# Down projection of a SwiGLU layer: four passes over two column blocks and half the rows, with some row tiles by seven products

## The chip, the cores and the metric

The kernel runs on one core of one Trainium2 chip. TensorE (PE) multiplies; VectorE (DVE) and ScalarE (ACT) prepare its operands and take its results out of PSUM; SyncE (SP) issues the loads of the weights, GpSimd (POOL) some other transfers. The time is that of one execution on the device, in microseconds. Three executions of the kernel before took 1140.74 (the median), 1136.53 and 1142.36.

## The reference

One decoder layer over 256 tokens of width 2048, in float32. The part that matters here is the feed-forward part with D_FF = 5632, and what surrounds it:

```python
x = x + mixed @ w_o[i]
hf = rms_norm(x, g_ffn_norm[i])
x = x + (jax.nn.silu(hf @ w_gate[i]) * (hf @ w_up[i])) @ w_down[i]
gate = jax.nn.sigmoid(rms_norm(x, g_ple_norm[i]) @ w_ple_gate[i])
x = x + gate * (p[i] @ w_ple_proj[i])
```

`w_down` is 5632 x 2048: 44 row tiles of 128 rows, and four column blocks of 512 columns.

## The kernel before, in words

**Products.** To keep float32 accuracy, each operand is split into a rounded high part and the rest (`w_hi`, `w_lo`; `gh`, `gl` for the gated values). A product of two such operands takes three matmuls: high by high, high by low, low by high. Tokens come as two tiles of 128 (t = 0, 1).

**Weights.** The class `Weights` cuts every weight matrix into chunks of two row tiles by up to 512 columns (512 KB), in the order in which they are used. `load_to` (line 163 on) issues the loads on SP, in order; a chunk goes into one of five buffers `raw`, or, of certain numbers below `more_end`, into one of two more buffers `w_more`. `split_to` makes `w_hi` on ACT (L200) and `w_lo` on DVE (L201); there are three buffers of each (PART). `take` keeps the splits and the loads ahead of the products.

**Seven products.** In gate/up, a chunk of `w_gate` and the chunk of `w_up` of the same rows form a pair. A pair of ordinary chunks needs eight block products of three matmuls. The up chunks in `W.mixed` are handled by `mix` (L206 on): sums of the four blocks of the pair (`w_sum`, L216), which are split (`w_last`, `w_mix`, L219 and L220), and `pair` (L1420) then makes seven block products in place of eight, with sums of the left operand (`rows`, made by `row_sums`, L1084). Four of the seven go into four shared PSUM banks (`pp_p`), the others into the four accumulators. `shared` (L1451) combines the four banks after the last such pair of a block, and the accumulators are added to that at the end of the block. In each of the 11 blocks of gate/up, four of eight pairs are of this kind (three in the first). Two sets of sum buffers (NSET) stand ready.

**Down.** Each of the four column blocks of `w_down` is one call of `block`: 22 chunks, each of 12 matmuls, into two of the four accumulators, so that the next block can start in the other two. Before the first chunks, `need_g` splits the gated values `gr` into `gh` and `gl`. After a block, `residual` (L1290) adds the accumulators to the tokens `xs`, and `norm_task` squares them, transposes them by PE and splits them into `ph`, `pl` for the last product (`ple`), between which and down lies the small product of `p` (`pp`).

**Order of the work.** The kernel is written as one list; a planner puts it in order for each engine at build time by simulated times and priorities. `high_priority` moves instructions ahead: the splits of the weights by 70 (W_AHEAD), the end of a gate/up block by 100 (G_AHEAD); the norm is put back by 100 (AHEAD). On the chip each engine then runs its own list in order, waiting on semaphores.

**Space.** Beside the weights' buffers there are 39 slots of 4 KB a partition (`S`), handed out first in, first out, and four PSUM banks (`PP`) beside the four accumulators.

## Time and profile before

| what | us |
|---|---|
| median of three runs | 1140.74 |
| lowest, highest | 1136.53, 1142.36 |
| the profiled execution's own time | 1135.29 |
| its span, first to last instruction | 1133.2 |
| gate/up blocks, from about | 320 to 785 |
| down blocks | 785 to 1028 |
| p product and last product | 1028 to 1128 |

The profile is of one execution. PE, DVE, ACT, POOL are busy times; PEld is the loading of the left operand, which runs beside the matmuls. Matmuls overlap, so one shows 0.39 us though the next starts after 0.23: a rate is read from the distance of starts. "L201" is line 201 of the kernel. A wait is written as who waited, and for whom: `DVE w_lo L201 <- ACT w_hi L200`. In the tables by stretch, each engine's busy time is followed by its number of instructions; then come the clock granted to PE (1.00 is full), the share of the DMA engines and GB/s.

### The profile page before, as it was taken

The numbers are of one execution on the slowest core, as the hardware profiler recorded it, in microseconds if no ns is written. First come the engines' busy times: TensorE is split into PE (matmuls) and PEld (weight loads), VectorE is DVE, ScalarE is ACT, GpSimd is POOL, SyncE is SP. The second block draws the span as 40 slices with busy tenths as digits, with TensorE's granted clock in tenths as the row PEclk, the third lists the DMA queues.
The fourth block names the chain that finished last, engine by engine and source line by source line (L and its number), as shares of the span: only waits on it lengthen the run. The fifth ranks groups of instructions, "written<-read, shape, count | busy, mean of one in ns | idle before, by whom it ended". The sixth has DMA issues, their size and how long they took to land.

```text
span 1133.2 us, 15659 instructions
## 1 busy us (share of the span) xinstructions
PE 1112.5 (98%) x5809; PEld 919.6 (81%) x5809; DVE 899.2 (79%) x1304; ACT 664.6 (59%) x946; POOL 23.3 (2%) x48
## 2 busy tenths in 40 slices
PE   9999999999999999999999999999999999999998
PEld 6877877889887878887887888888888888888886
DVE  7989998658799999999999999999744454546554
ACT  7864994636675766666665665667444343436443
POOL 1000020000000000000000000000000000000000
PEclk9999999999999999999999999999999999999999
DMA  9996470356685666666666665766665655555662
GB/s 336 242 271 202 115 237 23 108 189 201 194 275 180 196 196 185 211 201 183 212 201 183 217 204 176 223 218 198 197 193 187 195 188 192 186 195 187 211 212 86
DMA packets 113340, 221.16 MB, mean 195 GB/s; under 512 B 8160, under 2 KB 13040, under 8 KB 113264
## 3 DMA queue, kind: packets, MB, share of 16 engines
q1 hardware_dynamic: 109808, 211.23, 59.3%
q0 software_dynamic: 3456, 8.94, 2.5%
q8 instruction: 45, 0.74, 0.3%
q14 instruction: 31, 0.25, 0.1%
HBM read 214.76 MB, written 5.37 MB: 194 GB/s over the span
## 4 chain that ended last, share of the span: by engine, by line
PE 56%; DVE 28%; issue 6%; DMA 5%; ACT 3%; DVEq 0%; POOL 0%; SPq 0%; ACTq 0%; POOLq 0%
PE acc L371 48%; DVE w_lo L201 9%; DVE w_sum L216 7%; DMA w_raw<-in_w_up_dram 3%; DVE w_mix L220 3%; PE pp_p L371 3%; DVE uc L355 2%; DVE w_last L220 2%; DVE wsg L355 1%; DMA e<-in_bE_dram 1%; PE pp_at L371 1%; DVE w L763 1%; ACT w_hi L200 1%; PE pp_at L1016 1%; PE pp_v L744 1%
## 5 line engine op out<-in xcount | busy, mean ns | idle before, releaser
L201 DVE TENSOR_TENSOR w_lo<-w_raw,w_hi 128x1024 fp32r<-128x1024 f32 (+2 forms) x302 | 362.6, 1205 | 185.7 <-ACT w_hi L200 185.2
L200 ACT ACTIVATE w_hi<-w_raw 128x1024 fp32r<-128x1024 f32 (+2 forms) x302 | 314.6, 1044 | 291.1 <-PE acc L371 257.9
L371 PE MATMUL acc<-w_hi,fh 128*128 128x512 f32 x403 | 159.7, 396 | 0.1
L371 PE MATMUL acc<-w_lo,fh 128*128 128x512 f32 x403 | 158.3, 393 | 0.8
L371 PE MATMUL acc<-w_hi,fl 128*128 128x512 f32 x403 | 157.4, 391 | 0.0
L371 PE MATMUL acc<-w_hi,gh 128*128 128x512 f32 x352 | 137.6, 391 | 0.1
L371 PE MATMUL acc<-w_lo,gh 128*128 128x512 f32 x352 | 136.9, 389 | 0.0
L371 PE MATMUL acc<-w_hi,gl 128*128 128x512 f32 x352 | 136.9, 389 | 0.0
L219 ACT ACTIVATE w_mix<-w_sum 128x1024 fp32r<-128x1024 f32 x86 | 91.0, 1058 | 70.5 <-DVE w_sum L216 69.4
L220 DVE TENSOR_TENSOR w_mix<-w_sum,w_mix 128x1024 fp32r<-128x1024 f32 x86 | 104.8, 1219 | 0.3 <-ACT w_mix L219 0.2
L371 PE MATMUL pp_p<-w_mix,sum 128*128 128x512 f32 x387 | 95.3, 390 | 2.0 <-DVE fl L363 2.0
L371 PEld LDWEIGHTS acc<-w_lo,fh 128*128 128x128 f32 x403 | 76.0, 188 | 18.4 <-DVE w_lo L201 3.5
L371 PEld LDWEIGHTS acc<-w_hi,fh 128*128 128x128 f32 x403 | 75.8, 188 | 16.8 <-DVE uc L355 1.7
L371 PEld LDWEIGHTS acc<-w_hi,fl 128*128 128x128 f32 x403 | 75.9, 188 | 15.7
L371 PEld LDWEIGHTS pp_p<-w_mix,sum 128*128 128x128 f32 x387 | 72.4, 188 | 17.9 <-issue 2.4
L371 PEld LDWEIGHTS acc<-w_hi,gh 128*128 128x128 f32 x352 | 66.1, 188 | 14.0 <-DVE uc L355 0.4
L371 PEld LDWEIGHTS acc<-w_hi,gl 128*128 128x128 f32 x352 | 66.1, 188 | 13.8
L371 PEld LDWEIGHTS acc<-w_lo,gh 128*128 128x128 f32 x352 | 66.1, 188 | 13.7
L371 PE MATMUL acc<-w_hi,ph 128*128 128x512 f32 x128 | 49.8, 389 | 0.0
L371 PE MATMUL acc<-w_lo,ph 128*128 128x512 f32 x128 | 49.8, 389 | 0.0
L371 PE MATMUL acc<-w_hi,pl 128*128 128x512 f32 x128 | 49.8, 389 | 0.0
L200 ACT ACTIVATE w_hi<-w_more 128x1024 fp32r<-128x1024 f32 x37 | 39.0, 1054 | 14.5 <-PE acc L371 5.7
(318 smaller groups left out, 1906.9 us busy)
## 6 DMA issues: line engine op xcount, KB each, us to landing
w_raw<-in_w_down_dram SPq DMA_DIRECT2D x88, 512.0 KB, 4.3
w_raw<-in_w_gate_dram SPq DMA_DIRECT2D x64, 512.0 KB, 4.4
w_raw<-in_w_up_dram SPq DMA_DIRECT2D x63, 512.0 KB, 4.7
w_raw<-in_w_o_dram SPq DMA_DIRECT2D x32, 512.0 KB, 3.8
w_raw<-in_w_ple_gate_dram SPq DMA_DIRECT2D x32, 512.0 KB, 4.2
w_more<-in_w_up_dram SPq DMA_DIRECT2D x25, 512.0 KB, 4.6
w_raw<-in_w_in_dram SPq DMA_DIRECT2D x24, 512.0 KB, 7.7
w_more<-in_w_gate_dram SPq DMA_DIRECT2D x24, 512.0 KB, 4.3
```

The source lines that it names most:

```text
L200: self.nc.scalar.activation(out=hi, in_=raw, func=AF.Copy)
L201: self.nc.vector.tensor_tensor(out=lo, in0=raw, in1=hi.bitcast(F32), op=ALU.subtract)
L216: V.tensor_tensor(out=o, in0=a, in1=b, op=ALU.add)
L219: A.activation(out=h, in_=r, func=AF.Copy)
L220: V.tensor_tensor(out=l, in0=r, in1=h.bitcast(F32), op=ALU.subtract)
L355: V.tensor_tensor(out=o, in0=a, in1=b, op=op)
L371: T.matmul(out=o, lhsT=a, rhs=b, start=start, stop=stop)
L744: T.matmul(out=pv[p, r * 256 + i4 * 64:r * 256 + i4 * 64 + 64], lhsT=ee[r][p, i * 64:i * 64 + 64], rhs=um[p, i, :], start=True, stop=True, ...
L763: V.tensor_tensor_scan(out=w, data0=dc, data1=w, initial=0.0, op0=ALU.mult, op1=ALU.add)
L1016: T.matmul(out=o, lhsT=a, rhs=b_, start=False, stop=(i == 1), skip_group_check=True)
```

## The change

The down projection is computed by `mixed_block`, as gate/up is. There are four passes: for the first 20 row tiles (the first five gated tiles of four) the column blocks 0 and 1 together, then 2 and 3 together; then the same for the other 24 row tiles. A pair is two chunks of the same rows in two neighbouring column blocks. In each of two column pairs, seven of the 22 pairs of row tiles (D_MIXED: 3, 5, 8 in the first half, 13, 15, 17, 20 in the second) use seven products: 14 of 44. The gated values of a half are split when it comes up, and with them the sums of rows for the pairs in D_MIXED (`split_g`). Each pass uses all four accumulators, and ends with four combinations (`ws`, `uc`) and four additions to `xs`, so each column block is added to `xs` twice. The norm follows passes 2 and 3, for two column blocks at a time. The two `w_more` buffers are used up to the loads of gate/up block 8 only and their slots given back at block 9; gate 0 is split before block 10; the buffers of the sums are kept to the last pass.

```diff
-    blk["down"] = [W.block(w_down, 0, 44, 512 * b, 512) for b in range(4)]
+    D_MIXED, D_SPLIT = (3, 5, 8, 13, 15, 17, 20), 5
+    blk["down"] = []
+    for half in (range(2 * D_SPLIT), range(2 * D_SPLIT, 22)):
+        for p in range(2):
+            ids = [(j, *(W.block(w_down, 2 * j, 2, 1024 * p + c, 512)[0] for c in (0, 512))) for j in half]
+            W.mixed.update(i[2] for i in ids if i[0] in D_MIXED)
+            blk["down"].append(ids)
...
-    W.more_end = blk["down"][0][0]
+    W.more_end = blk["gu"][8][0][1]
     W.more.extend(wait_n(2, [128, 2, 512], "w_more"))
+    more = list(W.more)
     gr, gh, gl = [], [], []
+    lhs_g = tiles4(gh, gl)
...
     for b in range(11):
+        if b == 9:
+            S.put(*more)
+        if b == 10:
+            W.more.clear()
+            gh.append(wait_get([128, 4, 256], "gh", F32R))
+            gl.append(wait_get([128, 4, 256], "gl", F32R))
+            split(gh[0], gl[0], gr[0])
+            S.put(gr[0])
         ws = wsg[b % 2]
         acc = mixed_block(blk["gu"][b], lhs_f, rows, ws, uc, need_f)
...
-    S.put(*more, *fh, *fl, *rows.values(), uc, *w_sum)
-    for last, _, parts in W.sums:
-        S.put(last, *parts[0], *parts[1])
+    S.put(*fh, *fl, *rows.values(), wsg[1])
     for i in range(4):
         xs[i // 2][i % 2] = t = wait_get([128, 1024], "xs")
         nc.gpsimd.dma_start(out=t, in_=keep[i])
-    lhs_g = tiles4(gh, gl)
-
-    def need_g(k):
-        while len(gh) <= min(k // 4 + 1, 10):
+    rows = {}
+
+    def need_g(j):
+        last = D_SPLIT if j < 2 * D_SPLIT else 11
+        if n == 1 and j == 2 * D_SPLIT - 3:
+            split_g(D_SPLIT + 1)
+        split_g(min((j + 1) // 2 + 1, last))
+
+    def split_g(m):
+        while len(gh) < m:
             i = len(gh)
             sched.until(f"g{i}")
             gh.append(wait_get([128, 4, 256], "gh", F32R))
             gl.append(wait_get([128, 4, 256], "gl", F32R))
             split(gh[i], gl[i], gr[i])
+            for q in range(2):
+                if 2 * i + q in D_MIXED:
+                    w = wait_get([128, 512], "rows")
+                    o = rows[2 * i + q] = wait_get([128, 2, 512], "sum", F32R)
+                    row_sums((w, o[:, 0], o[:, 1]), gr[i][:, 2 * q:2 * q + 2].rearrange("p k n -> p (k n)"))
+                    S.put(w)
             S.put(gr[i])
...
-    for b in range(4):
-        ph.append(wait_get([128, 4, 256], "ph", F32R))
-        pl.append(wait_get([128, 4, 256], "pl", F32R))
-        acc = block(blk["down"][b], lhs_g, need_g)
-        residual(acc, r_f, b)
-        sched.add(norm_task(xv, b, ss_p, ph, pl, G_PLE, "hp"), 0)
-        if b == 0:
-            S.put(*wsg)
+    ws = wsg[0]
+    for n, ids in enumerate(blk["down"]):
+        p, h = n % 2, n // 2
+        acc = mixed_block(ids, lhs_g, rows, ws, uc, need_g)
+        with tc.high_priority(G_AHEAD):
+            for t in range(2):
+                tt(ws[:, t], ws[:, t], acc[2 * t], ALU.add)
+            for t in range(2):
+                tt(uc[:, t], acc[2 * t + 1], uc[:, t], ALU.subtract)
+        for c, o in enumerate((ws, uc)):
+            for t in range(2):
+                stt(xv(t, 2 * p + c), o[:, t], r_f[:, t:t + 1], xv(t, 2 * p + c))
+        if n == 3:
+            S.put(*gh[D_SPLIT:], *gl[D_SPLIT:], *(rows[j] for j in D_MIXED if j >= 2 * D_SPLIT), *w_sum)
+            for last, _, parts in W.sums:
+                S.put(last, *parts[0], *parts[1])
+        if h:
+            for b in (2 * p, 2 * p + 1):
+                ph.append(wait_get([128, 4, 256], "ph", F32R))
+                pl.append(wait_get([128, 4, 256], "pl", F32R))
+                sched.add(norm_task(xv, b, ss_p, ph, pl, G_PLE, "hp"), 0)
+        if n == 1:
+            S.put(*gh[:D_SPLIT], *gl[:D_SPLIT], *(rows[j] for j in D_MIXED if j < 2 * D_SPLIT))
+            pr_ = wait_get([128, 2, 2, 256], "prhl", F32R)
+            prh, prl = pr_[:, 0], pr_[:, 1]
             pr32 = wait_get([128, 2, 256], "pr32")
             nc.gpsimd.dma_start(out=pr32, in_=pT)
...
```

## The prediction, made before the changed kernel was run

> **What bounds the kernel now.** First the page: the engines' totals.

> ```profile
> span 1133.2 us, 15659 instructions
> PE 1112.5 (98%) x5809; PEld 919.6 (81%) x5809; DVE 899.2 (79%) x1304; ACT 664.6 (59%) x946; POOL 23.3 (2%) x48
> ```

> TensorE is busy in nearly the whole span, and VectorE for 79% of it. An average over stages hides which of the two is near its limit where, so next the busy time of each engine in stretches: two gate/up blocks of 42 us, then the four down blocks (columns: length, then PE, PEld, DVE, ACT, POOL).

> ```profile
> 414.00:456.00 42.00, 42.00 (x190) 34.49 (x188) 40.71 (x51) 26.26 (x30) 0.00 (x0) 1.00 0.65 198
> 456.00:498.00 42.00, 41.87 (x188) 34.11 (x187) 40.56 (x51) 26.23 (x30) 0.00 (x0) 1.00 0.64 198
> 785.00:846.00 61.00, 60.92 (x273) 50.05 (x272) 39.92 (x38) 26.62 (x28) 0.00 (x0) 1.00 0.59 188
> 846.00:907.00 61.00, 61.00 (x275) 50.57 (x274) 30.10 (x30) 26.02 (x30) 0.00 (x0) 1.00 0.60 191
> 907.00:968.00 61.00, 61.00 (x275) 50.57 (x274) 30.26 (x30) 26.02 (x30) 0.00 (x0) 1.00 0.59 191
> ```

> In gate/up, where four of eight pairs already use seven products, DVE is 97% busy (40.7 of 42). In down it is half idle (30 of 61). So down is bound by PE alone, and the change spends DVE's idle time there to save PE work. Third, the chain of waits in order of time gives the rates, because overlapping instructions show longer durations than their distance (columns: start, us, what).

> ```profile
> 623.09 1.14 DVE w_mix L220
> 627.10 1.20 DVE w_sum L216 x2
> 657.70 1.20 DVE uc L355 x2
> 742.26 1.21 DVE uc L355 x2
> 794.84 57.17 PE acc L371 x252
> 852.01 0.87 PE pp_n L398 x8
> 852.89 59.89 PE acc L371 x264
> ```

> A matmul of 512 columns takes 57.17/252 = 0.2269 us, a transpose 0.87/8 = 0.109. A 1024-wide DVE operation takes 1.14, a 512-wide one 0.60. A gate/up block lasts (742.26 - 657.70)/2 = 42.28 us (two periods lie between these rows); its PE work is 4x21 + 4x24 = 180 matmuls and 8 transposes, 41.71. A block at 97% DVE thus loses 0.57 us, while 264 down matmuls run without a gap.

> **The matmuls removed.** A pair by seven products has 21 matmuls, an ordinary one 24. That the form does so on the chip is in the page:

> ```profile
> L371 PE MATMUL pp_p<-w_mix,sum 128*128 128x512 f32 x387 | 95.3, 390 | 2.0 <-DVE fl L363 2.0
> L219 ACT ACTIVATE w_mix<-w_sum 128x1024 fp32r<-128x1024 f32 x86 | 91.0, 1058 | 70.5 <-DVE w_sum L216 69.4
> L220 DVE TENSOR_TENSOR w_mix<-w_sum,w_mix 128x1024 fp32r<-128x1024 f32 x86 | 104.8, 1219 | 0.3 <-ACT w_mix L219 0.2
> ```

> 86/2 = 43 pairs, 387/43 = 9 matmuls of three shared products each. Fourteen pairs save 14 x 3 = 42 matmuls, 42 x 0.2269 = **-9.53 us**. [...]

> **DVE in the four passes.** Each new pair replaces one ordinary split (1.14) by four sums, one half split and two splits: 5 x 0.60 + 2 x 1.14 = 5.28. Further rows:

> ```profile
> 1028.42 1.40 DVE L363 SCALAR_TENSOR_TENSOR xs<-acc,r_f,xs 128x512 f32<-128x512 f32 x2
> 1036.63 1.65 DVE L363 SCALAR_TENSOR_TENSOR pl<-pp_n,gc,ph 128x256 fp32r<-128x256 f32 x4
> L355 DVE TENSOR_TENSOR rows<-rows x16: 281/283/293, 304.3 to 340.3; 128x128 f32<-128x128 f32 x16
> L355 DVE TENSOR_TENSOR gl<-g,gh x11: 1219/1220/1222, 777.3 to 804.0; 128x1024 fp32r<-128x1024 f32 x11
> ```

> Residual 0.70 an operation, norm's lower half 0.41, a 128-wide sum about 0.21 (0.28 less the 0.07 by which the durations above exceed the distances); so row sums cost 4 x 0.21 + 0.60 = 1.44 for each of seven k positions. Each pass also has four shared sums (2.4) and, at its end, four combinations and four residuals (5.2), which run beside the next pass. The residual is made eight times more than before: +5.6 on DVE, under PE.
> - Pass 0: 17 split chunks 19.4, three mixes 15.8, shared 2.4, four gate splits 4.6, three row sums 4.3, block 10's end 3.6: 50.1. PE: 231 matmuls and 8 transposes, 53.3.
> - Pass 1: 19.4 + 15.8 + 2.4 + 5.2 + 1.1 (gate 5) + 0.6 (p) = 44.5. PE 52.4.
> - Pass 2: 20 chunks 22.8, four mixes 21.1, 2.4, 5.2, five gate splits 5.7, four row sums 5.8: 63.0. PE: 276 matmuls, 62.6.
> - Pass 3: 22.8 + 21.1 + 2.4 + 5.2 + 3.3 (norm of two column blocks) = 54.8. PE with 16 transposes 64.4.

> ACT has three copies of at most 1.06 and one of half the width in a new pair, 3.7 of its 4.8 us of PE, and less elsewhere, so DVE decides. Pass 2 alone asks for more than PE. Its relief: gate splits are planned as soon as their slots are free. The last row shows all eleven done by 804, while their block ran to 846. In pass 2 they take slots of gates 0 to 4, which pass 1 reads one after another, so some splits can move into pass 1 (8 us spare).

> **Stalls in the passes.** The trace has no such pass. Each is built like a gate/up block: all four accumulators in use, an ordinary pair last, ordinary pairs first, so that two of the accumulators are taken out while the last products still run. Nearest row: 0.57 a block. The bounds are 0 (down now) and 0.57 each for passes 0, 1 and 3; for pass 2 additionally 63.0/0.97 - 62.6 = 2.3 if nothing moves. I take 4 x 0.57 + 1.0 = **+3.3**, against at most 4.6.

> **The prefetch buffers.** `w_more` lends two buffers to the five of `raw`; the new limit stops it before block 8, since the 39 slots are full in block 10 (27 held by the stage, ten gates, two for `gh[0]` and `gl[0]`). Three blocks then mix at 97% DVE with five buffers. SP's loads wait for buffers, and DVE hardly for loads:

> ```profile
> SPq L174 <- DVE w_sum L216: 206.3, 70, 7.2
> SPq L174 <- DVE w_lo L201: 158.7, 93, 4.2
> DVE w_sum L216 <- DMA w_raw<-in_w_up_dram: 7.6, 8, 1.7
> DVE w_sum L216 <- DMA w_more<-in_w_up_dram: 1.1, 2, 0.6
> w_raw<-in_w_up_dram SPq DMA_DIRECT2D x63, 512.0 KB, 4.7
> ```

> One load shows what the two buffers do, the up chunk of a block's first mixed pair (instructions in order of time):

> ```profile
> 648.06 0.37 SPq L174 DMA_DIRECT2D w_more<-in_w_up_dram  x1
> 650.93 1.23 DVE L201 TENSOR_TENSOR w_lo<-w_raw,w_hi 128x1024 fp32r<-128x1024 f32 x1 [0.63 <-ACT w_hi L200]
> 652.81 0.69 DVE L216 TENSOR_TENSOR w_sum<-w_raw,w_more 128x512 f32<-128x512 f32 x1 [0.65 <-DMA w_more<-in_w_up_dram]
> ```

> It is used the moment it lands. Its pair starts two ordinary pairs (10.9) and the transposes (0.9) after the block's last accumulator is out (657.70 + 1.20), near 671, so 18 us later. With five buffers its issue waits for the chunk five before, whose last reader is the split ending at 652.16: it lands at 656.9, 4.1 us later. Queued behind it on SP are the next loads, on DVE its sums and those of the next mixed pair (they share `w_sum`). But DVE then has the block's ten end operations (6 us) to do, and the pair has 14 us left. DVE's spare is 3.3% of 42.28, 1.4 a block, so the bounds are 0 and 4.1 - 1.4 = 2.7 in each of three blocks, 0 to 8.1. DMA waits now cost DVE 8.7/11 = 0.8 a block; I let as much again arise and half reach PE: 3 x 0.4 = **+1.2**.

> **At no cost.** Bytes and size of the loads stay; POOL's reload of `xs` (four of 512 KB) and of `pT` lie 50 us before their use. The early split of gate 0 (1.14) falls into block 10, where four such splits fit already. The weight order changes between the column blocks only. The first new pair of pass 3 takes the four banks that norm uses, but 16.3 us into the pass (three ordinary pairs); norm's 3.3 on DVE is through by then. The end of down is the tight place:

> ```profile
> 1028.30:1040.00 11.70, 11.70 (x57) 9.77 (x56) 9.80 (x25) 10.30 (x19) 0.00 (x0) 1.00 0.60 195
> L367 ACT ACTIVATE pp_n<-xs 128x512 f32<-128x512 f32 x8 | 4.7, 582 | 0.0
> L367 ACT ACTIVATE ph<-pp_n,gc 128x256 fp32r<-128x256 f32 x12 | 4.7, 470 | 0.0
> ```

> ACT has 10.3 of 11.7 there, and gets two squares (0.58) and four copies (0.47) more, 3.0, since the last pass ends two column blocks at once. Their result isn't needed until eight row tiles into the last product, 10.9 after the p product. If the p product's own evictions are queued behind it, 10.3 + 3.0 - 11.7 = 1.6 is lost; I take **+0.3**, nearer to the cover.

> Sum: -9.53 + 3.3 + 1.2 + 0.3 = **-4.7 us**. The profiled execution took 1135.29 (span 1133.2 and 2.1 around it), which would become 1130.6. The three runs' median is 1140.74, 5.4 above it and within their spread of 1136.53 to 1142.36; on that scale the forecast is **1136.0**.

> **Rivals.**
> - *Clean (B).* The planner keeps DVE ahead throughout: stalls as in down now, 1 us in all. For it: passes 0, 1 and 3 are 85 to 94% full, below gate/up. Against: pass 2. Net -8.5: 1132.2.
> - *DVE sets the pace (C).* The seven-product pairs are there, but the saving becomes waiting: pass 2 +2.3, four ends 2.3, prefetch 3.0, tail 1.0; net -0.9: 1139.8. For it: DVE at 97 to 100%.
> - *Slower (D).* A stall long enough to slow PE's clock. The only large stall of gate/up shows it (PE in order of time; then one stretch: length, PE busy, granted clock, DMA share, GB/s):

> ```profile
> 340.82 0.39 PE L371 MATMUL acc<-w_hi,fl 128*128 128x512 f32 x1
> 343.26 0.93 PE L371 MATMUL pp_p<-w_mix,sum 128*128 128x512 f32 x3 [2.04 <-DVE fl L363]
> 345.58 0.63 PE L371 MATMUL acc<-w_hi,fl 128*128 128x512 f32 x1
> 346.00 0.63 PE L371 MATMUL pp_p<-w_hi,fh 128*128 128x512 f32 x1
> 344.60:348.00 3.40, 3.40 (x10) 0.51 0.09 9
> ```

> A distance of 2.44 instead of 0.23, and then 3.4 us at clock 0.51, in which half the work is lost: 2.2 + 1.7 = 3.9. Place: the mixed pairs of blocks 8, 9 and 10, whose sums come late with five buffers, and pass 2. One such stall in each is four, 15.6 in place of my 1.2 and 1.0: net +8.7, 1149.4. Without those two terms the sum is -6.9, so two stalls (+7.8) already make it slower than before, three give +4.8, four more than 0.5%. Against: 14 us of lead. [...] The trace halved the clock after a gap of 2.04, and D stays as priced.

> **How the numbers follow.** A measurement here tells about 0.5% (5.7 us) from no change. Forecast: 0.46; with stalls between 2.5 and 7 it spans -7 to -2.5 (1133.7 to 1138.2), and about 0.17 of it lies beyond -5.7. B 0.25, C 0.12, D 0.17. Faster 0.17 + 0.25 = 0.42; same 0.29 + 0.12 = 0.41; slower 0.17. The range takes in B and C, 3 us of the runs' spread below B, and D as far as three stalls (1145.5): 1129 to 1146.

> **What would show it.** Right: 42 fewer matmuls, down's matmuls ending about 5 us earlier counted from its first; DVE near 40 of 42 still in blocks 8 to 10, and no longer half idle but about 90% busy in the passes; no PE gap over 1 us. Wrong: PE waiting for `w_last` or `w_mix` behind DMA in blocks 8 to 10 (prefetch term), for `gl` or `sum` in pass 2 (pass term), clock below 1 between 400 us and the end of down (D), or gate/up blocks 8 to 10 as long as before and passes without gaps (B).

## The result, and the profile after

| | before | after |
|---|---|---|
| median of five runs (before: the first three stand above), us | 1140.74 | 1129.09 |
| lowest, highest | 1136.53, 1142.36 | 1126.46, 1130.01 |
| ratio after/before, 95% interval | | 0.9906 [0.9879, 0.9933] |
| profiled execution (span) | 1135.29 (1133.2) | 1129.42 (1127.7) |

The change makes the kernel about 0.9% faster. The medians are 11.65 us apart, the two profiled executions 5.9. A second series with 29 runs of the kernel before (after_again, below) gives a ratio of 0.9926 [0.9908, 0.9943]; of its median 1138.67 that is -8.4 us. That is the best figure of the three; why they differ is told further down.

First the engines' totals on the page of the kernel after, and the group of the shared products.

```profile
span 1127.7 us, 15773 instructions
PE 1103.1 (98%) x5767; PEld 911.7 (81%) x5767; DVE 987.9 (88%) x1463; ACT 692.8 (61%) x989; POOL 23.3 (2%) x48
L377 PE MATMUL pp_p<-w_mix,sum 128*128 128x512 f32 x513 | 126.4, 390 | 1.6 <-DVE fl L369 1.1
```

There are 42 matmuls fewer (5809 to 5767) and 513/9 = 57 pairs by seven products, 43 + 14. DVE has 89 us more to do, ACT 28. Where the time went is read from two groups of matmuls, that of gate/up (`fh`) and that of down (`gh`): count, durations, and the first and the last start. First of the kernel before, then of the kernel after.

```profile
L371 PE MATMUL acc<-w_hi,fh x403: 387/389/632, 315.7 to 784.5; 128*128 128x512 f32 x135
L371 PE MATMUL acc<-w_hi,gh x352: 389/389/497, 785.2 to 1028.0; 128*128 128x512 f32 x176
```

```profile
L377 PE MATMUL acc<-w_hi,fh x403: 387/389/500, 318.5 to 786.4; 128*128 128x512 f32 x135
L377 PE MATMUL acc<-w_hi,gh x254: 389/389/496, 787.1 to 1021.7; 128*128 128x512 f32 x127
```

Down, counted from its first to its last `gh` matmul, takes 234.6 us in place of 242.8: **-8.2**. (The expectations below count to the first matmul of the p product, 0.7 later.) Gate/up, from its first matmul to down's first, takes 468.6 in place of 469.5. From the last `gh` matmul to the end of the span there are 106.0 in place of 105.2. In the part ahead of gate/up, which the change does not touch, the kernel after happened to be slower: its first `fh` matmul starts at 318.5 in place of 315.7. That is why the two profiled executions lie only 5.9 apart. Now stretches of the kernel after: one gate/up block (block 8), then the four passes. Columns: length, then PE, PEld, DVE, ACT, POOL, each with its number of instructions; PE's clock, DMA share, GB/s.

```profile
667.00:709.00 42.00, 41.73 (x188) 34.28 (x187) 40.70 (x50) 26.27 (x30) 0.00 (x0) 1.00 0.63 197
...
787.00:840.00 53.00, 53.00 (x239) 43.81 (x238) 50.98 (x66) 31.33 (x36) 0.53 (x1) 1.00 0.63 209
840.00:893.00 53.00, 53.00 (x236) 43.89 (x235) 48.36 (x69) 31.75 (x36) 0.54 (x1) 1.00 0.62 203
893.00:957.00 64.00, 62.52 (x276) 51.44 (x275) 58.89 (x69) 34.79 (x39) 0.00 (x0) 1.00 0.61 197
957.00:1022.00 65.00, 64.50 (x293) 53.35 (x292) 55.75 (x70) 37.97 (x50) 0.00 (x0) 1.00 0.61 195
```

DVE is no longer half idle in down but 86 to 96% busy, and PE still has almost no hole: 1.48 and 0.50 us in 235. These two holes are the whole list of what PE waited for in down (who <- for whom: us in all, times, longest):

```profile
PE acc L377 <- DVE uc L361: 1.5, 1, 1.5
PE pp_p L377 <- DVE pl L369: 0.5, 1, 0.5
```

```profile
895.23 0.50 PE L377 MATMUL acc<-w_hi,gh 128*128 128x512 f32 x1 [1.48 <-DVE uc L361]
```

The first, at 893 to 895, is at the seam between the second and the third pass. VectorE in order of time there (start, us, operation):

```profile
880.78 0.28 DVE L361 TENSOR_TENSOR rows<-g 128x128 f32<-128x128 f32 x1
...
885.68 0.68 DVE L361 TENSOR_TENSOR rows<-g,rows 128x128 f32<-128x128 f32 x3
886.29 2.35 DVE L201 TENSOR_TENSOR w_lo<-w_raw,w_hi 128x1024 fp32r<-128x1024 f32 x2
888.56 0.68 DVE L361 TENSOR_TENSOR sum<-rows,sum 128x512 fp32r<-128x512 f32 x1
889.16 0.68 DVE L361 TENSOR_TENSOR uc<-wsg,pp_p 128x512 f32<-128x512 f32 x1
889.76 1.21 DVE L361 TENSOR_TENSOR gl<-g,gh 128x1024 fp32r<-128x1024 f32 x1
...
891.49 0.68 DVE L361 TENSOR_TENSOR wsg<-wsg,acc 128x512 f32<-128x512 f32 x1
...
892.70 0.74 DVE L369 SCALAR_TENSOR_TENSOR xs<-wsg,r_f,xs 128x512 f32<-128x512 f32 x1
893.36 1.21 DVE L201 TENSOR_TENSOR w_lo<-w_raw,w_hi 128x1024 fp32r<-128x1024 f32 x1
894.49 0.68 DVE L361 TENSOR_TENSOR uc<-acc,uc 128x512 f32<-128x512 f32 x1
```

Sixteen `rows` operations, the row sums of pairs 13, 15, 17 and 20, start between 880.8 and 886.1, with splits of weights among them. None of them is used before the third pass. Behind them come the combination of the shared banks (889.16) and, last, the one that empties the accumulator that PE wants (894.49, done at 895.17; PE goes on at 895.23). So the planner brought work of the third pass forward into the second, and the end of the second pass is late by it. That is the theory which the experiments test.

### The profile page after: what moved, and what is told of

Read it like the earlier page. It is cut to its first block, busy times and chain, and to the rows that moved or that the text cites. A ratio compares the mean times of both kernels' runs of the same rounds, so it can differ in the third digit from the quotient of the medians.

```text
span 1127.7 us, 15773 instructions
## 1 busy us (share of the span) xinstructions
PE 1103.1 (98%) x5767; PEld 911.7 (81%) x5767; DVE 987.9 (88%) x1463; ACT 692.8 (61%) x989; POOL 23.3 (2%) x48
## 4 chain that ended last, share of the span: by engine, by line
PE 46%; DVE 36%; issue 7%; DMA 7%; ACT 3%; DVEq 0%; POOL 0%; SPq 0%; ACTq 0%; POOLq 0%
PE acc L377 37%; DVE w_lo L201 12%; DVE w_sum L216 8%; PE pp_p L377 4%; DVE w_mix L220 4%; DMA w_raw<-in_w_up_dram 4%; DVE w_last L220 2%; DVE uc L361 2%; DVE wsg L361 2%; DMA e<-in_bE_dram 1%; PE pp_at L377 1%; ACT w_hi L200 1%; PE pp_at L1022 1%; DVE w L769 1%; DMA w_raw<-in_w_down_dram 1%
## 5 line engine op out<-in xcount | busy, mean ns | idle before, releaser
L200 ACT ACTIVATE w_hi<-w_raw 128x1024 fp32r<-128x1024 f32 (+2 forms) x299 | 310.6, 1043 | 216.3 <-PE acc L377 166.9
L201 DVE TENSOR_TENSOR w_lo<-w_raw,w_hi 128x1024 fp32r<-128x1024 f32 (+2 forms) x299 | 356.9, 1200 | 78.7 <-ACT w_hi L200 77.9
L219 ACT ACTIVATE w_mix<-w_sum 128x1024 fp32r<-128x1024 f32 x114 | 120.3, 1058 | 84.6 <-DVE w_sum L216 82.9
L220 DVE TENSOR_TENSOR w_mix<-w_sum,w_mix 128x1024 fp32r<-128x1024 f32 x114 | 138.5, 1216 | 0.1
L377 PE MATMUL pp_p<-w_mix,sum 128*128 128x512 f32 x513 | 126.4, 390 | 1.6 <-DVE fl L369 1.1
L377 PEld LDWEIGHTS pp_p<-w_mix,sum 128*128 128x128 f32 x513 | 96.0, 188 | 22.7 <-issue 2.4
L377 PE MATMUL acc<-w_hi,gh 128*128 128x512 f32 x254 | 99.1, 390 | 1.5 <-DVE uc L361 1.5
L377 PE MATMUL acc<-w_hi,gl 128*128 128x512 f32 x254 | 98.8, 389 | 0.0
L377 PE MATMUL acc<-w_lo,gh 128*128 128x512 f32 x254 | 98.8, 389 | 0.0
L216 DVE TENSOR_TENSOR w_sum<-w_raw 128x512 f32<-128x512 f32 x87 | 57.5, 682 | 13.3 <-DMA w_raw<-in_w_up_dram 5.9
L216 DVE TENSOR_TENSOR w_sum<-w_sum,w_raw 128x512 f32<-128x512 f32 x96 | 65.4, 681 | 0.0
L219 ACT ACTIVATE w_last<-w_raw 128x512 fp32r<-128x512 f32 x48 | 30.2, 628 | 32.6 <-DMA w_raw<-in_w_up_dram 16.8
## 6 DMA issues: line engine op xcount, KB each, us to landing
w_raw<-in_w_down_dram SPq DMA_DIRECT2D x88, 512.0 KB, 4.5
w_raw<-in_w_up_dram SPq DMA_DIRECT2D x71, 512.0 KB, 4.5
w_raw<-in_w_gate_dram SPq DMA_DIRECT2D x70, 512.0 KB, 4.5
w_raw<-in_w_o_dram SPq DMA_DIRECT2D x32, 512.0 KB, 4.0
w_raw<-in_w_ple_gate_dram SPq DMA_DIRECT2D x32, 512.0 KB, 4.5
w_raw<-in_w_in_dram SPq DMA_DIRECT2D x24, 512.0 KB, 7.5
w_more<-in_w_gate_dram SPq DMA_DIRECT2D x18, 512.0 KB, 4.3
w_more<-in_w_up_dram SPq DMA_DIRECT2D x17, 512.0 KB, 4.8
```

The lines of the kernel that those rows point to most:

```text
L200: self.nc.scalar.activation(out=hi, in_=raw, func=AF.Copy)
L201: self.nc.vector.tensor_tensor(out=lo, in0=raw, in1=hi.bitcast(F32), op=ALU.subtract)
L216: V.tensor_tensor(out=o, in0=a, in1=b, op=ALU.add)
L219: A.activation(out=h, in_=r, func=AF.Copy)
L220: V.tensor_tensor(out=l, in0=r, in1=h.bitcast(F32), op=ALU.subtract)
L377: T.matmul(out=o, lhsT=a, rhs=b, start=start, stop=stop)
```

## The experiments

All kernels were timed beside the kernel before on the same chip, in four series on four chips: the first four rows (the kernel before had a median of 1138.67 there), no_extra_buffers to pool_and_norm (1137.72), the next three (1138.88) and the last (1138.34). So ratios are compared, not medians. "Down" is the first to the last start of the `gh` group, as above.

| run | median, us (range, runs) | ratio to before, 95% | down, us |
|---|---|---|---|
| before_again | 1137.84 (1134.56 to 1141.17, 12) | 1.0003 [0.9989, 1.0017] | 242.9 |
| after_again | 1128.86 (1127.24 to 1130.11, 5) | 0.9926 [0.9908, 0.9943] | 234.5 |
| passes_only | 1137.29 (1135.42 to 1140.24, 12) | 0.9998 [0.9985, 1.0011] | 242.9 |
| less_prefetch | 1138.76 (1136.22 to 1141.60, 12) | 1.0007 [0.9993, 1.0021] | 243.4 |
| no_extra_buffers | 1143.02 (1140.03 to 1146.69, 9) | 1.0046 [1.0029, 1.0063] | 243.5 |
| norm_sooner | 1129.14 (1127.33 to 1129.76, 6) | 0.9919 [0.9902, 0.9936] | 234.1 |
| rows_on_pool | 1137.33 (1133.97 to 1141.12, 12) | 0.9992 [0.9978, 1.0006] | 241.8 |
| pool_and_norm | 1137.00 (1134.09 to 1141.45, 12) | 0.9994 [0.9979, 1.0009] | 241.6 |
| direct_residual | 1131.23 (1128.14 to 1133.90, 6) | 0.9933 [0.9912, 0.9954] | 235.1 |
| direct_and_norm | 1131.11 (1129.70 to 1135.46, 6) | 0.9940 [0.9922, 0.9957] | 238.7 |
| no_late_sums | 1128.34 (1126.65 to 1130.02, 2) | 0.9911 [0.9885, 0.9937] | 232.7 |
| late_rows_on_pool | 1129.47 (1127.23 to 1134.94, 9) | 0.9933 [0.9915, 0.9950] | 234.2 |

### The two kernels again

No edit; they give the spread and a second trace of each.

> The kernel before against itself. My theory: runs of one kernel spread over 3 to 6 us with the number of half-clock windows of 3.4 us that they meet (each costs 1.7 us), so the ratio is 1.000 within 0.002, and the granted clock orders the runs by time. The profile should again show a TensorE stall of over 2 us near 340 us, with or without the half-clock stretch behind it. Rival: the spread has nothing to do with the clock; then runs of one clock differ as much as runs of different clocks.

> The changed kernel once more, unaltered. My theory: the change is worth 42 matmuls (9.5 us) less about 2.4 us of stalls that the first profile shows in the passes, so some 7 to 8 us from the first gate/up matmul to the end; what the timed runs showed beyond that (11.6 us between the medians, 5.9 between the two profiled executions) is how the two kernels' executions happened to meet half-clock windows, and differs again here. I expect a ratio of 0.991 to 0.995. Rival: the change gains 11 us or more steadily, by something that the profiles do not show; then the ratio is 0.9905 or lower again.

Down repeats to 0.1 us in both kernels (242.8 and 242.9; 234.6 and 234.5), though their whole times vary by 5 us and more. The same hole stands at the same seam again:

```profile
PE acc L377 <- DVE uc L361: 1.7, 1, 1.7
```

So what down saves is steady, 8.2 and 8.5 us in the two pairs of traces (0.8 of it comes back behind down, see below), and the spread of a kernel's time comes from elsewhere. The two traces of the kernel before differ by 5.3 us in span; of that 4.2 lie ahead of gate/up (its first `fh` matmul starts at 315.7 and 319.9) and 1.0 in gate/up. The stall near 340 us was expected to be over 2 us again, and was 1.3 (1.56 from start to start, less 0.23).

### The parts of the change by themselves

passes_only keeps the order of the passes, the shorter prefetch and the late slots, but has no pair by seven products; with nothing to combine, the accumulators go straight to `xs`:

```diff
-    D_MIXED, D_SPLIT = (3, 5, 8, 13, 15, 17, 20), 5
+    D_MIXED, D_SPLIT = (), 5
...
-            for t in range(2):
-                tt(ws[:, t], ws[:, t], acc[2 * t], ALU.add)
-            for t in range(2):
-                tt(uc[:, t], acc[2 * t + 1], uc[:, t], ALU.subtract)
-        for c, o in enumerate((ws, uc)):
-            for t in range(2):
-                stt(xv(t, 2 * p + c), o[:, t], r_f[:, t:t + 1], xv(t, 2 * p + c))
+            for c in range(2):
+                for t in range(2):
+                    stt(xv(t, 2 * p + c), acc[2 * t + c], r_f[:, t:t + 1], xv(t, 2 * p + c))
```

> The four passes over two column blocks and half the rows without any pair of seven products in down; the residual is taken from the accumulators directly. All else as changed (slots, prefetch limit, splits of the gated values by halves). My theory: the gain is the 42 matmuls; they are back here (+9.5 us), and most of the 2.4 us of stalls go with the sums, so it ends within 2 us of the kernel before: ratio 0.998 to 1.002. Rival (order of the passes, of the loads, or the freed prefetch is worth something by itself): 3 to 5 us below the kernel before, 0.996 or lower.

Its time is that of the kernel before, and down takes 242.9. PE's waits in its down are one:

```profile
PE acc L377 <- DVE uc L361: 1.0, 1, 1.0
```

It stands 2.9 us behind the start of down, where the last combinations of gate/up empty the accumulators that the first pass wants. It hides that eight transposes (0.87) have left down, as told below. At the ends of the passes there is no wait: four accumulators in use, two additions to `xs` for each column block and the norm for two blocks at once cost nothing that can be seen there or behind down. The gain is that of the fourteen pairs. Why the kernel after does not have the wait of 1.0 stays open.

less_prefetch is the kernel before with the new limit of the extra load buffers alone; no_extra_buffers has them nowhere in gate/up (`W.more_end = 0`):

```diff
-    W.more_end = blk["down"][0][0]
+    W.more_end = blk["gu"][8][0][1]
```

> The kernel before with one line changed: the two extra weight buffers are used only up to the loads of gate/up block 8. My prediction priced this at +1.2 us (bounds 0 to 8.1), rival D at stalls of 3.9 us in each of blocks 8 to 10. The changed kernel's first profile shows blocks 8 and 9 at 41.7 and 42.4 us against 42.2 and 42.2 before, so I now expect 0 within 0.7 us (ratio 0.9995 to 1.0005, blocks 8 and 9 at 41.7 to 42.6 us). Rival: five buffers cost 0.4 us or more a block when the down stage behind has no early gate split (ratio 1.001 or more).

> The kernel before without the two extra weight buffers in all of gate/up (their slots stay taken). My prediction let five buffers cost 0.4 us in each of three blocks; the run with less prefetch showed nothing for three blocks. Theory now: VectorE has each pair's sums done so early (18 us ahead) that loads landing 4 us later are still in time: 0 to 1 us over eleven blocks (ratio 0.999 to 1.001), blocks 1 to 9 at 42.2 to 42.8 us as now. Rival: the cost is real but small for three blocks, 0.4 a block: 4.4 us over eleven (ratio 1.004).

The shorter use costs nothing measurable: 1.0007 [0.9993, 1.0021]. That interval alone would still admit the 1.2 us of the prediction; the traces are sharper. Blocks 8 to 10, cut by counting their matmuls, take 129.1 us together with the shorter use, against 128.6 and 129.5 in the two traces of the kernel before, and 128.3 and 128.8 in those of the kernel after. Without the buffers altogether the time grows by 0.46%, 5.2 us, where 0 to 1 was expected. Its waits of VectorE in gate/up, and the largest of them in order of time:

```profile
DVE w_sum L216 <- DMA w_raw<-in_w_up_dram: 19.8, 11, 5.3
```

```profile
331.74 0.69 DVE L216 TENSOR_TENSOR w_sum<-w_raw 128x512 f32<-128x512 f32 x1 [5.27 <-DMA w_raw<-in_w_up_dram]
```

The kernel before waits 7.6 + 1.1 us there (rows in the prediction). A quarter of the waiting is one load in the first block, where gate/up starts. Block 0 takes 46.9 us there, against 44.5 and 42.0 in the two traces of the kernel before (the first of them with a half-clock stretch of 3.4 us in it), and the other ten blocks together 429.7, against 425.0 and 428.5. So the extra buffers are worth something, most clearly in block 0, and nothing that can be measured in the last three.

### The stall at the seam: the norm, and GpSimd

norm_sooner lets the norm of the third pass's column blocks keep its place in the planner's order. rows_on_pool moves all 28 row sums of `row_sums` from VectorE to GpSimd. pool_and_norm does both.

```diff
+                AHEAD["norm_task"] = 0 if n == 2 else -100
                 sched.add(norm_task(xv, b, ss_p, ph, pl, G_PLE, "hp"), 0)
```

```diff
-        tt(s[0], a22, a21, ALU.subtract)
-        tt(s[2], a11, a21, ALU.subtract)
-        tt(s[1], a11, s[0], ALU.add)
-        tt(s[3], a12, s[1], ALU.subtract)
+        add(s[0], a22, a21, ALU.subtract)
+        add(s[2], a11, a21, ALU.subtract)
+        add(s[1], a11, s[0], ALU.add)
+        add(s[3], a12, s[1], ALU.subtract)
...
+    def on_pool(o, a, b, op):
+        nc.gpsimd.tensor_tensor(out=o, in0=a, in1=b, op=op)
...
```

> The changed kernel with the norm behind the third pass at normal priority in place of 100 back. The fourth pass's first seven-product pair takes the PSUM banks that the norm used, and waited 0.5 to 0.7 us for the norm's last subtraction in the first profile (0.3 in the second). My theory: that wait goes, nothing else changes: down 235.2 to 234.6 us. Rival: the norm brought forward delays the splits of the weights, and PE waits as long elsewhere in the fourth pass (down 235.0 to 236.5).

> The changed kernel with the 28 sums of rows (128 wide, four for each of seven positions) moved from VectorE to GpSimd; everything else is left to the planner. My theory of the stall at the end of the second pass (1.6 to 1.8 us in both profiles): the planner put 16 of these sums (3.3 us) and gate splits into the end of that pass, ahead of the combinations that free the accumulators, and VectorE ran behind the plan there. Then the stall falls below 0.5 us and down (from its first matmul to the p product's first) goes from 235.2 to 233.5 to 234.2 us. Rival: the end of a pass itself costs this (four shared sums, four combinations in 5.4 us), or VectorE's load of weights: the stall stays at 1.2 us or more. Second rival: GpSimd is slow enough that sums come late for pair 13 or 20: a new stall in the third pass.

> Both edits together, the candidate for a faster kernel: down 233.0 to 234.0 us against 235.2, ratio to the kernel before 0.990 to 0.9925, 1 to 2 us below the changed kernel. Rival: as the two single edits' rivals; then no gain over the changed kernel.

norm_sooner removes the smaller hole (PE's waits in down show only the one of 1.5 us) and down gets 0.5 us shorter. In the time this can't be told from nothing.

rows_on_pool loses the whole gain. Its stall begins at the first sum on GpSimd (GpSimd in order of time; each line is two sums):

```profile
775.91 6.49 POOL L1541 TENSOR_TENSOR rows<-g 128x128 f32<-128x128 f32 x2 [8.82 <-PE pp_p L377]
...
787.72 0.87 POOL L1541 TENSOR_TENSOR rows<-g 128x128 f32<-128x128 f32 x2
```

The first two sums show 6.49 us together. All other pairs of sums take 0.87 to 2.84, against 0.20 a sum from start to start on VectorE above. Why the first is so long is not shown. In late_rows_on_pool (below), where GpSimd had waited 18.9 us before them, the first two take 0.88, and there is no stall at the start of down.

At the start of down it is ACT, which evicts and splits for everybody, that waits for the sums. Behind it a split of VectorE (`w_lo`) waits 3.5 us for ACT's part, and behind that in VectorE's order stands the operation that empties PE's accumulator (ACT in order of time; PE's waits; then PE's clock by stretch):

```profile
784.37 0.63 ACT L373 ACTIVATE sum<-rows 128x512 fp32r<-128x512 f32 x1 [4.57 <-POOL rows L1541]
787.79 1.06 ACT L373 ACTIVATE gh<-g 128x1024 fp32r<-128x1024 f32 x1 [2.79 <-POOL rows L1541]
```

```profile
PE acc L377 <- DVE uc L361: 4.9, 2, 4.8
PE acc L377 <- DVE w_lo L201: 0.8, 1, 0.8
```

```profile
787.00:790.40 3.40, 0.55 (x3) 0.12 (x1) 0.00 (x0) 2.61 (x4) 2.94 (x7) 1.00 0.14 57
790.50:793.90 3.40, 1.58 (x4) 1.30 (x5) 3.40 (x5) 1.37 (x2) 0.00 (x0) 0.50 0.66 196
794.00:797.40 3.40, 3.40 (x10) 2.62 (x10) 2.52 (x5) 1.78 (x2) 0.00 (x0) 0.51 0.38 137
```

A stall of 4.8 us, and then 6.8 us at half clock, in the first half of which PE still stood for 1.8: it loses half of the other 5.0, 2.5 us. Together that is 7.3, and its down is 7.2 longer than that of the kernel after. At the seam itself the wait for `uc` is down to 0.16 (the smaller of the two in the row), as the theory expected, but 0.8 for a split (`w_lo`) stands in the second pass instead. In pool_and_norm the two are 0.98 and 0.20. So the sums on GpSimd take most of the wait away in one run and a third of it in the other, and leave 1.0 to 1.2 us of waiting in place of 1.48: too little to decide on the theory.

### The stall at the seam: a shorter end of the pass

direct_residual takes the accumulators out faster: the four operations that empty them add them to `xs` at once, and the shared sums follow (`r_n` is `-r_f`). The number of operations on VectorE in a pass is the same. direct_and_norm is that with norm_sooner's line.

```diff
-            for t in range(2):
-                tt(ws[:, t], ws[:, t], acc[2 * t], ALU.add)
-            for t in range(2):
-                tt(uc[:, t], acc[2 * t + 1], uc[:, t], ALU.subtract)
-        for c, o in enumerate((ws, uc)):
+            for c in range(2):
+                for t in range(2):
+                    stt(xv(t, 2 * p + c), acc[2 * t + c], r_f[:, t:t + 1], xv(t, 2 * p + c))
+        for c, (o, s) in enumerate(((ws, r_f), (uc, r_n))):
             for t in range(2):
-                stt(xv(t, 2 * p + c), o[:, t], r_f[:, t:t + 1], xv(t, 2 * p + c))
+                stt(xv(t, 2 * p + c), o[:, t], s[:, t:t + 1], xv(t, 2 * p + c))
...
```

> The changed kernel, but the accumulators of a pass are added to the tokens directly (four operations of 0.70 us, ahead), and the combined shared sums after that (with the factor negated for the second pair); before, the accumulators were first added to the shared sums, so they came free only behind the four shared operations. One operation's length more per pass, no other work. Theory 1 (the accumulators are freed late because they wait behind the shared sums): the 1.6 to 1.8 us stall at the end of the second pass falls below 0.5 and down goes from 235.2 to 233.5 to 234.2 us. Theory 2 (VectorE is simply behind there, by the sums of rows and gate splits put ahead): the stall stays at 1.2 us or more.

> The same with the norm behind the third pass at normal priority (worth 0.4 us by itself in down). The candidate for a faster kernel. Theory 1: down 233.2 to 233.9 us, ratio to the kernel before 0.9905 to 0.992. Theory 2: 234.4 to 235.0, ratio as the changed kernel's.

The wait for `uc` is gone, as theory 1 had it, but others have come and down is no shorter, as theory 2 had it: neither expectation holds whole. PE's waits of direct_residual in down:

```profile
PE pp_p L377 <- DVE pl L369: 1.0, 1, 1.0
PE acc L377 <- DVE w_lo L201: 0.8, 2, 0.4
```

DVE has as much to do as before, and the lateness shows at whatever it serves next. Behind down it is 1.0 us longer than the kernel after (107.0 against 106.0). In direct_and_norm one wait for `w_lo` is 1.4 us, and behind one of the moved stalls the clock halved (PE in order of time, then by stretch):

```profile
986.23 1.08 PE L377 MATMUL pp_p<-w_mix,sum 128*128 128x512 f32 x3 [1.81 <-DVE pl L369]
```

```profile
986.90:990.30 3.40, 3.40 (x10) 2.62 (x9) 3.40 (x6) 0.63 (x1) 0.00 (x0) 0.50 0.42 157
```

Its down took 238.7: 1.97 us of waiting (2.20 from start to start, less 0.23) and 1.7 lost at half clock.

### The stall at the seam: without the sums

no_late_sums takes the suspected work away: pairs 13, 15, 17 and 20 use the sums of pair 3, all matmuls stay. Its values are not the layer's; it is for the time alone.

```diff
-                if 2 * i + q in D_MIXED:
+                if 2 * i + q >= 2 * D_SPLIT:
+                    rows[2 * i + q] = rows[3]
+                elif 2 * i + q in D_MIXED:
...
```

> The changed kernel without the sums of rows of the second half: the four pairs 13, 15, 17 and 20 use the sums of pair 3 in place of their own, so 16 sums of 128 columns, four copies and four subtractions of 512 columns are left out, and those pairs' values are not the layer's. It takes 5.8 us of VectorE's work away, of which some 4 us stand at the end of the second pass. Theory 2 (VectorE behind by this work): the stall at the second pass's end falls below 0.6 us, down to 233.3 to 234.3. Theory 1 (order of freeing): it stays above 1.0 us.

PE's only wait in down, then the third pass by stretch, then DVE in order of time at the seam:

```profile
PE pp_p L377 <- DVE pl L369: 0.5, 1, 0.5
```

```profile
893.00:957.00 64.00, 64.00 (x284) 52.97 (x284) 56.26 (x65) 34.54 (x40) 0.00 (x0) 1.00 0.63 203
```

```profile
886.08 0.69 DVE L361 TENSOR_TENSOR uc<-wsg,pp_p 128x512 f32<-128x512 f32 x1
...
891.80 1.28 DVE L361 TENSOR_TENSOR uc<-acc,uc 128x512 f32<-128x512 f32 x2
```

Times of two traces are compared from the start of each one's down (787.12 in the kernel after, 786.12 here). So counted, the combination starts at 99.96 instead of 102.04, 2.1 us earlier, and the emptying of the accumulator at 105.68 instead of 107.37, 1.7 us earlier. The sums took about 3.3; part of that VectorE now spends waiting. The hole is gone, and down is 1.8 us shorter (232.7 against 234.6). So this work, pulled forward, is what makes the end of the second pass late. Of the 1.8, the hole is 1.64 (1.87 from start to start, less 0.23), 0.11 the next distance on PE, which was 0.335 in place of 0.227, and 0.05 the other hole.

### The late sums alone on GpSimd

If only the four late pairs' sums go to GpSimd, none stands in ACT's way at the start of down. This run has norm_sooner's line too.

```diff
-                    row_sums((w, o[:, 0], o[:, 1]), gr[i][:, 2 * q:2 * q + 2].rearrange("p k n -> p (k n)"))
+                    row_sums((w, o[:, 0], o[:, 1]), gr[i][:, 2 * q:2 * q + 2].rearrange("p k n -> p (k n)"),
+                             on_pool if i >= D_SPLIT else None)
...
+                AHEAD["norm_task"] = 0 if n == 2 else -100
```

> The changed kernel with two edits: the row sums of the second half's four pairs (13, 15, 17, 20) go to GpSimd, those of the first half stay on DVE; and the norm of pass 2's two column blocks is no longer put back in the planner's order. Nothing is left out. Theory 1 (the 3.3 us of sums on DVE at the end of the second pass are the stall, and GpSimd's work slows DVE as much as it relieves it): 16 sums of about 1.05 us on GpSimd slow DVE's operations beside them by 20 to 40%, 3 to 5 us of DVE, as much as the sums took; the stall at the end of the second pass is moved or smaller, down stays at 234.3 to 236 us, and the time is that of the changed kernel (1128 to 1130). Rival (GpSimd's slowing of DVE costs little where DVE isn't full): the stall near 893 is gone as in the kernel without these sums, down takes 233.0 to 234.0, and the time is 1.5 to 2 us below the changed kernel's. A first-pass stall of 5 us as with all the sums on GpSimd appears in neither.

Down takes 234.2 with it and 234.1 without (norm_sooner): nothing gained. The stall has moved to 880, in the midst of the sums. VectorE in order of time, one operation before GpSimd's sums (870 to 887), two beside them and one after, then PE:

```profile
860.09 0.68 DVE L216 TENSOR_TENSOR w_sum<-w_sum,w_raw 128x512 f32<-128x512 f32 x1
...
874.02 0.95 DVE L216 TENSOR_TENSOR w_sum<-w_sum,w_raw 128x512 f32<-128x512 f32 x1
...
878.57 1.48 DVE L201 TENSOR_TENSOR w_lo<-w_raw,w_hi 128x1024 fp32r<-128x1024 f32 x1
...
892.00 1.22 DVE L201 TENSOR_TENSOR w_lo<-w_raw,w_hi 128x1024 fp32r<-128x1024 f32 x1
```

```profile
880.10 0.50 PE L377 MATMUL acc<-w_lo,gh 128*128 128x512 f32 x1 [1.15 <-DVE w_lo L201]
```

The same split takes 1.48 in place of 1.22 while GpSimd adds, and the same sum of 512 columns 0.95 in place of 0.68. GpSimd works some 15 us on the sums (the second pass by stretch):

```profile
840.00:893.00 53.00, 51.85 (x229) 42.60 (x228) 48.36 (x52) 30.88 (x36) 15.06 (x17) 1.00 0.60 203
```

Twelve operations of VectorE are lengthened in these, by 3.1 us together, against 3.3 us of sums taken off it. VectorE is busy for 48.36 us of this stretch, exactly as in the kernel after, with 17 operations fewer. No complete version tried here beats the changed kernel by more than the noise.

## Why the prediction was right, and where it was not

The sign came out, and 1129.09 lies 0.09 us above the lower end of the range. That it lies inside is luck in part. The forecast itself, -4.7, is below the 0.5% that counts as a change; "faster" had 0.42 against 0.41 for "same", and more than half of the 0.42 came from rival B. The size is nearer to that of B (-8.5) than to the forecast. B had down without new stalls, 1 us in all; the runs show 2.2 and no other cost.

- **The matmuls removed, -9.53: right.** 42 matmuls fewer at an unchanged rate (0.227 us; 60 in 13.62 from 791.05 on in the trace after), and passes_only shows that nothing else in the change gains.
- **The transposes.** The sum left out that they move. Of the norm's 32 transposes 24 lay within down, 8 behind each of three blocks; now there are 16, and 16 behind it (the chain of waits of the kernel after in order of time):

```profile
962.87 1.75 PE pp_n L404 x16
...
1027.97 1.75 PE pp_n L404 x16
```

  So 8 x 0.109 = 0.87 leave the stretch of down and stand behind it, and explain the 0.8 by which the end grew (450 matmuls and transposes there in place of 442).
- **DVE in the four passes: right in size.** Forecast 50.1, 44.5, 63.0, 54.8; the stretches show 51.0, 48.4, 58.9, 55.8. Some 4 us moved from the third pass into the second, as the prediction said they could. It named gate splits as what moves, and did not ask what that work would push back.
- **Stalls in the passes, +3.3: too large and misplaced.** "4 x 0.57 + 1.0" became 2.2 (9.53 + 0.87 - 8.2). Three of the four ends show no wait, so the end's build alone does not cost the 0.57 of a gate/up block. That a DVE 97% busy over the whole block does is likely, and not shown here. The third pass itself, the one that alone asked for more than PE, has no wait behind its first matmul. The one large stall is at the end of the second pass, 1.64, because of the relief itself, as no_late_sums shows.
- **"Norm's 3.3 on DVE is through by then": wrong,** though it costs only 0.5 us of waiting in one trace and 0.1 in the other. Norm is put back in the planner's order, so its lower halves (`pl`) are still being made when the first new pair of the last pass asks for the banks. norm_sooner shows it: there the wait is gone.
- **Prefetch, +1.2: not there.** The prediction let new waits of DVE arise and half of them reach PE. less_prefetch shows no loss in blocks 8 to 10, and gate/up is 468.6 and 469.7 us in the two traces after, against 469.5 and 470.5 before. The 14 us of lead that the prediction names would explain it; no run tests that by itself.
- **The tail, +0.3: nothing** beyond the transposes.
- **Rival C** (DVE sets the pace) asked for holes in all passes, and PE is busy in 233.0 of 235.0. **Rival D** (a stall that halves the clock) did not come: the clock is 1.00 in all stretches of down, and the only hole of note was 1.48. But rows_on_pool and direct_and_norm show such stalls in down, at a price of 7.3 us (4.8 and 2.5) and of 3.7 (1.97 and 1.7). The kernel after is not far from it: its stall at the seam is 1.64 in one trace and 1.83 in the other, against 1.97 in direct_and_norm.
- **The scale of the median.** The forecast was set on 1140.74. Over 29 later runs the kernel before has a median of 1138.67, so part of the 11.65 is a high start. With the steps as measured, -9.53 + 2.2 + 0 + 0 = -7.3; the second series gives -8.4, with an interval of -10.5 to -6.5, and the two agree within it.

## What to carry to other kernels

Work moved onto an engine with room is free only if what it displaces isn't due: beside the sum over a stage, ask what the planner will bring forward into the free time and which short, urgent operation (here the emptying of an accumulator) then stands behind it. Removing one such wait while the engine's load stays moves the lateness to its next customer, so test a cause by taking the work away. And compare stages by their own length in the trace: down repeated to 0.1 us, where whole times spread by 5.

## What the runs showed of the hardware

```profile
185.92 0.95 PE L404 MATMUL pp_at<-ident,att_p 128*128 128x128 f32 x3 [2.14 <-DVE att_p L365]
```

```profile
186.10:189.50 3.40, 3.40 (x15) 3.14 (x15) 3.40 (x7) 1.33 (x3) 0.00 (x0) 0.50 0.00 0
```

```profile
186.43 0.70 PE L404 MATMUL pp_at<-ident,att_p 128*128 128x128 f32 x3 [2.14 <-DVE att_p L365]
```

```profile
186.10:189.50 3.40, 2.96 (x20) 2.31 (x20) 3.40 (x9) 1.86 (x5) 0.00 (x0) 1.00 0.00 0
```

Counted in multiples of 3.413 us from the half-clock starts of its execution, the first gap (the distance of two starts, 2.41 us, less 0.23 as idle time) lies with all its 2.18 us between two of them, 182.65 and 186.06. That a multiple cuts the second gap in two is the author's estimate, and not shown. In the traces before and after, of all distances over 1.3 us between 75 and 1100 us, the four with 1.97, 2.15, 2.18 and 2.68 us of idle time between two multiples were followed by half clock, and none with up to 1.64 was. (What a stretch already at half clock needs to come back isn't settled: in rows_on_pool one in which PE was busy for 1.58 of 3.40 us was followed by another at half.) At half clock a matmul of 512 columns starts every 0.43 us in place of 0.23 (the trace after, 90.63 to 93.19), and a stretch in which PE is busy costs about half its length, 1.7 us. As the same wait was followed by one in one execution and not in another, this is one source of the spread of these times (over 41 executions of the kernel before, time and mean granted clock correlate by -0.69, about half of the variance; the rest stays open, and in its two traces most of the difference lies ahead of gate/up, while the longer one has the higher mean clock, 0.998 against 0.995). At the seam 1.64 us was followed by clock 1.00 (the stretch from 893.00 above holds it), and 1.97 us in direct_and_norm by 0.50.

**GpSimd beside VectorE.** Beside additions on GpSimd, VectorE's operations with two inputs took 1.48 us in place of 1.22 at 1024 columns and 0.95 in place of 0.68 at 512 (late_rows_on_pool, as quoted). The price is 0.26 to 0.27 us an operation at either width, 21% of the wider and 40% of the narrower. GpSimd's sums were lengthened too: in rows_on_pool two take 0.87 us at 787.72, where VectorE is idle (0.00 us busy from 787.00 to 790.40, above), and as much as 2.84 us at 886.65, beside VectorE's operations.
